# Moving a LayerNorm from the first stages of each pass into the merges of the same pass, by way of DRAM, with new ranks and filler matmuls

## The chip, the cores and the metric

One Trainium2 chip, all eight cores; each core computes one of the eight batch elements with the same program. The metric is the device time of the slowest core in microseconds (us). Some executions of any kernel here are in a slower state, in which the cores of one die or of both are granted a lower matrix-engine clock (0.87 on one die and 0.985 on the other in one slow run of the changed kernel). Ratios are the mean time of one kernel's fast runs over that of the other's of the same rounds, so they are not quite the ratio of the medians.

## The reference, cut to what matters

```python
def hybrid_layer(x, ...):                       # two layers, x is (8, 2048, 2048)
    h = x * (1 + scale) + shift                 # mixer input
    proj = h @ w_in
    ys = (ssd_branch(...), swa_branch(...), shortconv_branch(...), rglru_branch(...))
    m = sum_k sigmoid(proj_gate[k] + b_gate[k]) * (ys[k] @ w_branch[k])
    out = m @ w_out
    return layer_norm(ALPHA * x + gate * out, ln_w, ln_b)
```

## The kernel before

The kernel is a list scheduler written in Python. Parts of the computation are generators that add operations with a rank ("key"); the program simulates the five engines and the DMAs, always takes the ready operation of lowest rank, and so fixes the order of instructions on each engine. The traces show each engine keeping to one order (in the trace of this kernel ACT's 4518 and POOL's 563 instructions come in the same sequence on all eight cores, DVE's 6902 but for two swapped pairs of neighbours on a core at most): where the program believes that a DMA lands earlier than it does, the engine stands at the instruction that needs the data.

A core makes four passes: layer 1 on the first and second half of the sequence, then layer 2 on both. A pass has the stages short convolution and recurrence (the "first stages"), SSD (the state-space branch), attention, merges, output projection. While a pass merges its branches, the mixer input of the next pass is made in eight chunks (`h_chunk`). After the output projection come the statistics of the norm, and then, during the first stages of the *next* pass, the norm itself:

```python
def out_unit(n):
    ...
    for dc in range(NKC):                        # 16 blocks of 128 channels x 1024 tokens
        r, rr, tr = alloc([TU], F32)
        R[dc] = (r, tr.r, tr)                    # kept in SBUF until normalised
        ... yield from out_mm(...)               # r = x + gate * (m @ w_out), and sums
    ... ln_stats(part, rs, ms)
    for dc in range(NKC):
        ln_apply(l, u, dc, 0, TU, R[dc], rs, trs.r, ms, tms.r)   # 2 DVE, 1 ACT, 1 store
        yield P.key + LNSTEP                     # one every 7 us of rank
def h_chunk(n, j, direct):
    ...
        P.dma("sp", xt, src[u, kc], ...)         # src = x1, the normalised input of layer 2
        P.key += HL                              # rank what uses it HL later
        for h, b in enumerate((b0, b1)):
            act(o[b], xt[:, h * T:(h + 1) * T], AF.Identity, ..., scale=..., bias=...)
```

The softmax here doesn't subtract the row's maximum and nothing guards it: scores larger than these inputs give would overflow.

## Time and profile before

| | |
|---|---|
| time, median of 3 | 5880.87 us (5874.19 to 5884.1) |
| profiled execution | 5853.3 us, 5822.8 to 5853.3 over the cores |
| matrix engine (PE) busy | 5497.7 us |
| vector engine (DVE) busy | 4178.1 us |
| bytes moved by DMA | 856.94 MB |

The lines are in the prediction. ACT is the scalar engine, POOL is GpSimd, and SP is the sync engine, which issues most of the DMAs (1238 of 1728 in the trace of the kernel before). A row of a cut by stretches has, after the stretch, its length, then busy microseconds of PE, weight loads, DVE, ACT and POOL with instruction counts, then the granted clock, the busy share of the 16 DMA engines and GB/s.

### The profile page before, as it was taken

The page shows a single profiled execution, that of the slowest core. Times are in us where ns is not written, and L with a number is a line of the kernel's source. Part 1 is how long each engine was busy: PE and PEld are TensorE (multiplying, and loading weights), DVE is VectorE, ACT ScalarE, POOL GpSimd, SP SyncE. Part 2 cuts the span into 40 slices and gives each one's busy share as a digit, 9 for nine tenths or more (in the row PEclk, how much of TensorE's full clock was granted, in tenths as well). Part 3 has the DMA queues.
Part 4 walks back from the last instruction along what each step waited for, and adds up shares of the span by engine and source line. Part 5 has one row for each costly group of instructions (what it writes and reads, how often), then busy time and mean ns, then how long its engine had stood idle before and what let it go on. Part 6 is the DMA issues. An engine that isn't in the chain of part 4 may idle for free.

```text
span 5853.3 us, 84743 instructions; the slowest of 8 cores (5822.8 to 5853.3 us)
## 1 busy us (share of the span) xinstructions
PE 5497.7 (94%) x28129; PEld 2545.5 (43%) x28680; DVE 4178.1 (71%) x6902; ACT 2835.4 (48%) x4518; POOL 322.9 (6%) x563
## 2 busy tenths in 40 slices
PE   1999899899999999989999999999999999999998
PEld 1444344444444444444443444444444444444445
DVE  7787776666698788766578776766658777766556
ACT  1565654433266566443236566644324656645224
POOL 0000000000000000000000000000000000000004
PEclk9999999999999999999999999999999999999999
DMA  9567777576576677767566666766856556665554
GB/s 306 115 129 142 134 141 162 132 181 158 176 176 130 137 143 142 162 159 168 143 194 155 122 123 123 130 131 143 181 163 168 107 93 116 114 140 119 127 116 151
DMA packets 251823, 856.94 MB, mean 146 GB/s; under 512 B 27776, under 2 KB 91392, under 8 KB 206848
## 3 DMA queue, kind: packets, MB, share of 16 engines
q0 software_dynamic: 64672, 411.20, 40.7%
q1 hardware_dynamic: 184416, 423.51, 24.1%
q10 hardware_dynamic: 2304, 16.78, 0.9%
q8 instruction: 234, 3.83, 0.3%
q14 instruction: 197, 1.61, 0.1%
HBM read 1133.32 MB, written 120.85 MB: 214 GB/s over the span
## 4 chain that ended last, share of the span: by engine, by line
PE 78%; DMA 10%; DVE 5%; issue 4%; ACT 3%; SPq 1%; DVEq 0%; ACTq 0%; POOL 0%; POOLq 0%
PE ps L736 77%; DVE arena L709 3%; ACT arena L705 3%; DMA arena<-cum_scr 2%; DVE arena L713 2%; DMA arena<-arena 2%; DMA yd_scr<-arena 1%; DMA arena<-w_ada 1%; DMA arena<-wb 1%; PE ps L741 1%; DMA arena<-w 1%; DMA arena<-x 1%; SPq L329 1%; DMA arena<-x_scr 1%; ACT L705 0%
## 5 line engine op out<-in xcount | busy, mean ns | idle before, releaser
L736 PE MATMUL ps<-arena 128*128 128x512 bf16 (+6 forms) x27425 | 5472.5, 363 | 328.9 <-DVE arena L713 103.9
L736 PEld LDWEIGHTS ps<-arena 128*128 128x128 bf16 (+4 forms) x27976 | 2487.0, 100 | 3223.8 <-issue 612.5
L709 DVE TENSOR_TENSOR arena<-arena 128x1024 bf16<-128x1024 bf16 (+8 forms) x3052 | 1998.6, 693 | 297.2 <-ACT arena L705 176.5
L705 ACT ACTIVATE arena<-arena 128x512 f32<-128x512 f32 (+9 forms) x2356 | 1395.6, 633 | 1383.3 <-DVE arena L709 789.4
L709 DVE TENSOR_TENSOR arena<-ps,arena 128x512 f32<-128x512 f32 (+5 forms) x1491 | 708.9, 494 | 536.6 <-PE ps L736 469.4
L705 ACT ACTIVATE arena<-ps 128x512 f32<-128x512 f32 (+5 forms) x838 | 533.7, 644 | 666.8 <-PE ps L736 556.4
L713 DVE SCALAR_TENSOR_TENSOR arena<-arena 128x1024 f32<-128x1024 f32 (+2 forms) x765 | 760.1, 1009 | 92.4 <-ACT arena L705 56.7
L713 DVE SCALAR_TENSOR_TENSOR arena<-arena,ps 128x512 f32<-128x512 f32 (+1 forms) x640 | 405.9, 645 | 508.8 <-PE ps L736 428.6
L705 ACT ACTIVATE ps<-ps 128x512 f32<-128x512 f32 x624 | 363.7, 583 | 525.2 <-PE ps L736 492.6
L705 ACT ACTIVATE arena<-ps,arena 128x512 f32<-128x512 f32 (+1 forms) x456 | 311.9, 684 | 325.1 <-PE ps L736 297.5
L705 ACT ACT_TABLE_LOAD x238 | 305.4, 1283 | 89.9 <-DVE arena L709 38.6
L329 POOL DMA_DIRECT2D arena<-w x184 | 97.7, 531 | 2635.7 <-PE ps L736 1986.6
L713 DVE SCALAR_TENSOR_TENSOR arena<-ps,arena 128x512 f32<-128x512 f32 (+1 forms) x153 | 104.7, 687 | 157.3 <-PE ps L736 156.4
L329 POOL DMA_DIRECT2D arena<-wg x128 | 67.7, 529 | 1999.4 <-PE ps L736 1908.1
L709 DVE TENSOR_TENSOR ps<-ps,arena 128x512 f32<-128x512 f32 (+1 forms) x222 | 147.6, 665 | 14.1 <-DVE arena L713 0.5
L741 PE MATMUL ps<-arena 128*128 128x128 bf16 (+1 forms) x704 | 101.0, 243 | 10.2 <-DVE arena L709 5.3
L329 POOL DMA_DIRECT2D arena<-wb x128 | 67.9, 531 | 730.3 <-DVE arena L709 357.4
L741 PEld LDWEIGHTS ps<-arena 128*128 128x128 bf16 (+1 forms) x704 | 69.4, 115 | 67.2 <-issue 26.1
L709 DVE TENSOR_TENSOR arena<-arena,ps 128x256 f32<-128x256 f32 (+1 forms) x172 | 75.3, 450 | 22.0 <-PE ps L736 18.1
L727 DVE RECIPROCAL arena<-arena 128x4 f32<-128x4 f32 (+3 forms) x144 | 72.3, 504 | 15.0 <-ACT arena L705 8.5
L709 POOL TENSOR_TENSOR arena<-arena 128x256 f32<-128x256 f32 (+1 forms) x81 | 71.4, 907 | 95.0 <-ACT arena L705 94.4
L1604 DVE TENSOR_TENSOR_SCAN arena<-arena 128x1024 f32<-128x1024 f32 x32 | 74.1, 2317 | 0.5
(18 smaller groups left out, 85.1 us busy)
## 6 DMA issues: line engine op xcount, KB each, us to landing
arena<-w POOLq DMA_DIRECT2D x184, 1024.0 KB, 10.1
arena<-wg POOLq DMA_DIRECT2D x128, 1024.0 KB, 10.1
arena<-w_ada SPq DMA_DIRECT2D x128, 512.0 KB, 8.0
arena<-wb POOLq DMA_DIRECT2D x128, 512.0 KB, 10.6
arena<-x SPq DMA_DIRECT2D x64, 512.0 KB, 5.8
mp_scr<-arena SPq DMA_DIRECT2D x64, 512.0 KB, 8.6
arena<-cum_scr SPq DMA_DIRECT2D x128, 256.0 KB, 7.5
arena<-mp_scr SPq DMA_DIRECT2D x64, 512.0 KB, 9.9
```

What stands on the lines that cost most here:

```text
L329: eng.dma_start(out=o.fn[0], in_=o.fn[1]).then_inc(s, 16)
L705: return P.op("act", lambda e: e.activation(out=out, in_=in_, func=func, **kw), reads, writes, cost=cost, acc=acc, tbl=tbl, hi=hi)
L709: return P.op(eng, lambda e: e.tensor_tensor(out=out, in0=in0, in1=in1, op=op), reads, writes, cost=0.2 + n * 2.1e-3 if eng == "pool" else ...
L713: return P.op("dve", lambda e: e.scalar_tensor_tensor(out=out, in0=in0, scalar=scalar, in1=in1, op0=op0, op1=op1), reads, writes, cost=c_d ...
L727: P.op("dve", lambda e: e.reciprocal(out=out, in_=in_), reads, writes, cost=0.13 + n * 6.3e-3)
L736: r = e.matmul(out, lhsT=lhsT, rhs=rhs, start=st, stop=sp_, skip_group_check=True)
L741: P.op("pe", lambda e: e.transpose(out=out, in_=in_, identity=ident), reads, writes, cost=cost, acc=acc)
L1604: P.op("dve", lambda e: e.tensor_tensor_scan(out=c, data0=a, data1=xs, initial=init, op0=ALU.mult, op1=ALU.add), [ra, rxs] + ri, cv.r, cos ...
```

## The change

The intent is to take the norm of the pass before out of the first stages, where DVE is busiest, and put it into the merges, where the next mixer input is made. The unnormalised blocks go to DRAM at once and their SBUF is free. The scale (128 x 1024 fp32) lies meanwhile in the SSD state buffer, which is not used between the last SSD of one pass and the first of the next; for one pass the state is saved to DRAM and fetched back. The change also retunes ranks and adds filler matmuls that should keep the PE clock up. Core of the diff:

```diff
@@ out_unit
-            R[dc] = (r, tr.r, tr)
+            P.dma("sp", raw[n, dc], r, reads=tr.r, writes=[rRAW[n][dc]], nbytes=524288)
+            mem.free(tr)
-        for dc in range(NKC):
-            ln_apply(l, u, dc, 0, TU, R[dc], rs, trs.r, ms, tms.r)
+        for i, (v, r) in enumerate(((rs, trs.r), (ms, tms.r))):
+            P.dma("sp", lns[n, i], v, ...)
@@ h_chunk, layer 2
+                for h, b in enumerate((b0, b1)):
+                    xt, rx, tx = alloc([T], F32)
+                    P.dma("sp", xt, raw[n - 2, kc][:, lo], ..., nbytes=262144, hi=4.0)
+                    P.key += HL
+                    normalise(0, n - 2, kc, xt, rx, h * T, T)             # 2 DVE, 1 ACT
+                    P.dma("sp", x1[u, kc][:, lo], xt, ..., nbytes=262144)
+                    act(o[b], xt, AF.Identity, ...)
+    def ln_out(m): ...    # pass 3's norm, whose result is the output, in pass 4's merges
-    ROPEL, HL, ADAL = 0.0, 6.0, 15.0
+    ROPEL, HL, ADAL = 4.0, 10.0, 15.0
+    order = P.warm(order, ...)    # bursts of 3 filler matmuls into idle banks, in gaps
+                                  # that the program's own simulation shows
... (cut: loading and freeing the scale, spacing constants, bookkeeping)
```

## The prediction

> **What bounds the kernel now.** I read the page's busy shares first, then the chain that ended last, then busy time by stage, then the waits inside the stages that lose time, and last the clock.
>
> ```profile
> span 5853.3 us, 84743 instructions; the slowest of 8 cores (5822.8 to 5853.3 us)
> PE 5497.7 (94%) x28129; PEld 2545.5 (43%) x28680; DVE 4178.1 (71%) x6902; ACT 2835.4 (48%) x4518; POOL 322.9 (6%) x563
> PE 78%; DMA 10%; DVE 5%; issue 4%; ACT 3%; SPq 1%; DVEq 0%; ACTq 0%; POOL 0%; POOLq 0%
> ```
>
> The matrix engine (PE) is the bound: 94% busy, 78% of the chain. All that a change of elementwise work or buffers can win is its idle time, 5853.3 - 5497.7 = 356 us, and the time it runs on a slowed clock. The program makes four passes (two layers by two halves of the sequence), each with five stages: short convolution and recurrence, SSD, attention, merges, output projection. Cut at these stages (columns: busy us of each engine with its count, granted clock, DMA share, GB/s):
>
> ```profile
> 150.00:470.00 320.00, 317.55 (x1504) 139.22 (x1533) 247.31 (x361) 186.57 (x263) 16.43 (x31) 1.00 0.64 125
> 1155.00:1460.00 305.00, 296.04 (x1536) 137.58 (x1566) 188.40 (x343) 101.74 (x152) 15.30 (x29) 0.99 0.74 171
> 1460.00:1595.00 135.00, 133.66 (x614) 60.81 (x623) 77.69 (x110) 26.02 (x42) 1.05 (x2) 1.00 0.55 178
> 1595.00:1905.00 310.00, 301.20 (x1407) 131.52 (x1437) 281.10 (x356) 196.21 (x275) 12.68 (x24) 1.00 0.68 150
> 3028.00:3345.00 317.00, 304.94 (x1415) 132.89 (x1444) 268.30 (x343) 198.46 (x265) 15.79 (x30) 0.99 0.65 139
> 4450.00:4765.00 315.00, 310.74 (x1450) 135.63 (x1479) 256.35 (x304) 200.07 (x279) 13.73 (x26) 1.00 0.57 113
> 5450.00:5745.00 295.00, 293.58 (x1345) 133.83 (x1370) 157.07 (x240) 69.30 (x106) 19.51 (x30) 1.00 0.54 135
> ```
>
> Rows 1, 4, 5 and 6 are the first stage of passes 1 to 4. Pass 1 has no norm to apply; passes 2 to 4 apply the norm of the pass before. DVE rises from 247 to 281 us (91% of the stage) in pass 2, and PE idle goes from 2.5 us to 8.8, 12.1 and 4.3 us. The merges (rows 2 and 7) leave DVE at 62% and 53%. So the norm sits where DVE is scarcest, but it costs PE only about 25.2 - 3 x 2.5 = 18 us in all three passes.
>
> What the extra DVE work is shows in the groups of pass 2's first stage; its first-pass counterpart has 15 such instructions, not 46:
>
> ```profile
> L709 DVE TENSOR_TENSOR arena<-arena 128x1024 f32<-128x1024 f32 x46 | 56.0, 1229 | 2.3 <-ACT arena L705 2.3
> ```
>
> The rest of the idle time lies elsewhere. The same arithmetic on the cuts of the other stages gives 107 us in the four SSD stages, 53 us in attention, 23 in the merges, and 123 us before the first dense matmul. In attention DVE stands still behind the DMAs that turn halves of q and k for the rotary embedding, and PE behind DVE (first row from the waits of 2345 to 2600, the others DVE and PE in order of time):
>
> ```profile
> DVE arena L709 <- DMA arena<-arena: 12.7, 5, 7.8
> 2581.32 1.23 DVE L709 TENSOR_TENSOR arena<-arena 128x1024 f32<-128x1024 f32 x1 [7.75 <-DMA arena<-arena]
> 2583.49 6.86 PE L736 MATMUL ps<-arena 128*128 128x65 bf16 x30 [8.22 <-DVE arena L709]
> 2578.50:2585.00 6.50, 1.51 (x11) 0.88 (x12) 3.68 (x7) 0.00 (x0) 0.00 (x0) 0.50 0.67 241
> ```
>
> The last row is a cut inside that wait: the granted clock is 0.50. The clock record has 21 such stretches of 3.41 to 10.24 us between 500 us and 5430 us, each after a PE gap. Counting the columns of the matmuls that started in them, at half speed against full, gives 47 us lost.
>
> [...] stretches are multiples of 3.41 us, and dense 128x512 matmuls start 216 ns apart at full clock. [...] The trace has 1229 and 688 to 691. It follows that cutting a 1024-wide operation in two costs 0.15 us. [...] The trace has a 128 KB on-chip copy at 5.7 us to landing[...].
>
> **The change part by part.**
> (1) Norm out of the first stages. Removed from passes 2 to 4 each: 32 DVE operations x 1.225 = 39 us, 16 ACT operations x 1.16 = 19 us, 16 stores of 512 KB. It also ends the hold on 16 tiles of 4 KB per partition across the boundary. Gain on PE: the 18 us above, and the one slowed stretch at 3100 us, 2.4 us. Together -20 us.
> (2) Norm into the merges. Merges of passes 2 and 3 gain 64 half-width operations x 0.69 = 44 us of DVE each, and 32 ACT operations x about 0.70 = 22 us. DVE goes from 188 to about 232 of 305 us, 76%, well below the 91% above. They also get 8.4 MB of stores of the normalised input; the load of it is only swapped for the raw one. The hardware queue's 24.1% of 5853 us for 423.5 MB is 3.33 us of all 16 engines per MB, so 28 us, and the share goes from 0.74 to 0.83. Pass 4's merges get 39 us DVE and 16.8 MB, share 0.54 to 0.73. DVE works in order, so a late raw load can block it and with it the merge arithmetic; but these operations are ranked 10 instead of 6 behind their load. I put +2 us a pass, +6 us.
> (3) Raw stores in the output stages: 8.4 MB, 28 us of all engines in 133, so the share goes from about 0.57 to 0.78 beside the loads of w_out, x and h. Nothing waits for these stores. +2 us. Statistics and the saved state add 6.8 MB in all, nothing.
> (4) The state buffer holds the scale only between the last SSD of one pass and the first of the next. Its save and restore are off the path. 0.
> (5) Retuned ranks: the rotary multiplications are ranked 4 later. Their stalls above 3 us cost PE 3.2 + 3.3 + 4.5 + 8.2 = 19 us and 11 us in slowed clock. In the built order the typical distance on DVE from writing q to rotating it hardly grows (about 12 to 13 instructions); only the shortest (1 and 2) go to 5. I count a third of 30: -10 us.
> (6) Filler matmuls. The order of the changed program has 240 more 128x512 matmuls, in 80 bursts of 3: 47 bursts before the dense work and 33 later. A burst is 0.65 us at 216 ns, so at most 33 x 0.65 = 21 us if the gaps they were planned for are not there on the chip. I found some 35 gaps of over 1.4 us in the trace; the 33 bursts stand in 18 places. If half of the places meet a real gap, each saves about 2.2 us (47/21), so -20, and half of the bursts cost 11. Net -9 us. In the opening the slowed stretch at 131 to 151 us cost 2.1 us: -2 us.
> Sum: -20 + 6 + 2 - 10 - 9 - 2 = -33 us, 0.6%. 5881 - 33 = 5848; I say 5846.
>
> **The rivals.** (a) Nothing shows: PE's idle time moves with the schedule. All instructions are placed anew, and the SSD gaps (107 us, several behind loads of the cumulative decay and not touched by the change) may fall either way by 20 us. That gives 5860 to 5885. For it: the moved work was mostly hidden already. (b) The merges become the new jam: DVE blocked by raw loads that land late at share 0.83, weights of the merges late for PE. PE already waited for such weights at 630 and 876 us. A 5 us stall in each of 8 chunks x 2 passes would be +80 us, giving 5930. Against it: DVE at 76%, loads issued ahead, and before the same loads of x held ACT up in the merges for only 2.5 us. (c) The fillers work better than I think and the attention stalls vanish: -20 - 30 - 35, giving 5790. Against it: the fillers stand where the program expects gaps, and the largest gaps come from DMAs that land later than it expects.
>
> **Range and chances.** Predicted 5846 us, 8 times in 10 within 5800 to 5890. Faster by over 2% means below 5763, which would need 118 us, a third of all idle time and far beyond the parts above: 0.05. Slower by over 2%, above 5998, needs (b) in full: 0.03. Within 2%: 0.92.
>
> **What would show it.** Right if: DVE busy in the first stages of passes 2 to 4 falls by about 39 us each and PE idle there to 2 to 4 us; DVE in the merges rises to about 76% with PE idle there at most 3 us more a pass; bytes rise by some 40 MB; fewer than 18 slowed stretches; waits of DVE for the rotary DMAs shrink. Wrong if: PE in the merges waits for weights or for DVE behind raw loads, if slowed stretches stay at 21 while PE gains 20 us of busy time (fillers in gaps that are not there), or if the SSD gaps move by more than the rest together.

The sum stays -20 + 6 + 2 - 10 - 9 - 2 = -33 us, and its 1.225, 0.69 and 1.16 us an operation and 216 ns a matmul are measured in the trace. "1229 and 688 to 691" are ns of an fp32 TENSOR_TENSOR of 1024 and of 512 columns. On the clock the trace of the kernel before (core 6) shows this: each of the 21 slowed stretches begins 0.6 to 4.8 us after the start of a PE gap of 1.7 us or more, and 128x512 matmuls start 427 ns apart in such stretches (median) against 216 outside. That a filler in a gap saves the stretch was my estimate from that, not shown.

## The result, and the profile after

The fast runs of the changed kernel took 5893.61 and 5904.16 us (two more, 5960 and 6502 us, were slow; the median of all four is 5932.12 us). Before took 5874.19 to 5884.1 us. The ratio is 1.0032 with a 95% interval of 1.0008 to 1.0056: slightly slower, where I had predicted 0.6% faster. It is within 2% all the same.

The page of the changed kernel, its busy and chain lines and the group of the fillers:

```profile
span 5892.1 us, 85799 instructions; the slowest of 8 cores (5850.3 to 5892.1 us)
PE 5575.6 (95%) x28361; PEld 2565.6 (44%) x28920; DVE 4178.1 (71%) x6966; ACT 2851.4 (48%) x4551; POOL 323.2 (5%) x563
PE 78%; DMA 11%; DVE 5%; issue 4%; ACT 2%; SPq 1%; DVEq 0%; ACTq 0%; POOL 0%; POOLq 0%
L2379 PE MATMUL ps<-arena 128*128 128x512 bf16 x229 | 81.5, 496 | 59.0 <-DVE arena L797 30.8
```

PE is "busier" only because of the fillers (81.5 us). The bound and the chain are nearly the same. Bytes rose by 41.0 MB, as forecast ("some 40"). Slowed stretches between 500 and 5430 us did not fall below 18: there are 28 on this core, and 22.5 in the mean over the cores against 20.9 before.

The cuts of the first stages of passes 2, 3 and 4, and of pass 2's merges with output; then pass 2's wide fp32 operations in its first stages, and its attention waits for the rotary copies:

```profile
1612.00:1922.00 310.00, 308.03 (x1449) 135.99 (x1476) 254.23 (x335) 181.84 (x263) 13.35 (x25) 1.00 0.62 134
3060.00:3377.00 317.00, 315.11 (x1476) 138.65 (x1504) 241.12 (x323) 184.06 (x255) 16.84 (x32) 1.00 0.63 127
4479.00:4794.00 315.00, 312.95 (x1463) 137.10 (x1492) 225.46 (x278) 183.37 (x265) 13.74 (x26) 1.00 0.49 94
2640.90:3060.70 419.80, 399.59 (x1912) 181.77 (x1949) 273.19 (x453) 132.97 (x201) 14.25 (x27) 0.98 0.82 204
...
L793 DVE TENSOR_TENSOR arena<-arena 128x1024 f32<-128x1024 f32 x15 | 18.3, 1220 | 1.3 <-ACT arena L789 1.3
...
DVE arena L793 <- DMA arena<-arena: 4.2, 4, 1.2
```

PE in the first stages went as predicted: idle 8.8 to 2.0 us, 12.1 to 1.9, 4.3 to 2.1. The 46 wide operations are 15. DVE's busy time fell from 281 to 254 us, 268 to 241 and 256 to 225, so by 27 to 31 us and not by 39: the wide operations that left pass 2 make up 37.7 us, so some 11 us of other DVE work moved in. The merges did not go as predicted. The same stretch of the kernel before, from pass 2's last attention matmul to its norm statistics:

```profile
2626.10:3027.80 401.70, 394.86 (x1922) 181.67 (x1958) 239.99 (x394) 109.78 (x170) 14.25 (x27) 1.00 0.68 172
```

It has grown by 18 us, DMA share rose from 0.68 to 0.82, and PE idle from 6.8 to 20.2 us though DVE is busy only 65% of the time. The waits of the changed kernel show why: first DVE's waits in this stretch, then DVE, ACT and PE in order of time around 2850 us, then the cut around it.

```profile
DVE arena L793 <- DMA arena<-raw_scr: 23.5, 8, 8.2
...
2855.78 0.69 DVE L793 TENSOR_TENSOR arena<-arena 128x512 f32<-128x512 f32 x1 [8.15 <-DMA arena<-raw_scr]
2857.76 0.81 ACT L789 ACTIVATE arena<-arena 128x512 f32<-128x512 f32 x1 [9.01 <-DVE arena L793]
2859.21 3.15 PE L820 MATMUL ps<-arena 128*128 128x512 bf16 x7 [6.34 <-ACT ps L789]
...
2840.00:2860.00 20.00, 12.58 (x69) 5.38 (x69) 11.85 (x23) 5.73 (x9) 1.05 (x2) 0.94 0.97 196
```

Read the three engines as one chain. DVE stood 8.15 us at one norm multiplication because its raw block had not landed. ACT waited 9.01 us for DVE, and PE 6.34 us for a bank of PSUM (`ps`, where it writes its output) with which ACT had not finished. The DMA engines were 97% busy in these 20 us; of what the trace shows, only they had no room left. A full stretch alone does not stop PE: two other cuts of 20 us, from 2700 and from 2820 us, have shares of 1.04 and 1.03 (a transfer is booked where it starts), and PE idle is 0.1 us in each.

To see the whole run I cut each core's trace at events that both kernels have: the statistics matmul that ends SSD, the last attention matmul, the statistics matmul of the norm. The table has the mean length over all eight cores of one profiled execution, in us; columns 3 to 6 belong to the experiments below.

| stretch | before | changed | e1 | e10 | e11 | e14 |
|---|---|---|---|---|---|---|
| pass 1 first stages + SSD | 914.6 | 923.2 | 915.3 | 928.3 | 926.0 | 919.1 |
| pass 2 first stages + SSD | 756.8 | 745.0 | 746.6 | 750.2 | 756.4 | 754.0 |
| pass 3 first stages + SSD | 736.4 | 725.6 | 726.2 | 728.4 | 737.2 | 740.5 |
| pass 4 first stages + SSD | 717.3 | 727.3 | 730.0 | 731.9 | 719.2 | 731.4 |
| attention, all passes | 1091.6 | 1094.1 | 1090.8 | 1094.5 | 1093.3 | 1096.2 |
| pass 1 merges + output | 399.4 | 401.2 | 400.7 | 399.6 | 400.4 | 399.3 |
| pass 2 merges + output | 399.3 | 414.1 | 413.7 | 401.1 | 415.3 | 399.3 |
| pass 3 merges + output | 398.9 | 418.6 | 421.9 | 408.5 | 412.7 | 398.1 |
| pass 4 merges | 345.7 | 340.2 | 340.2 | 340.2 | 345.7 | 345.6 |
| tail | 76.1 | 75.9 | 75.8 | 77.6 | 76.0 | 75.4 |
| whole | 5836.1 | 5865.2 | 5861.3 | 5860.1 | 5882.1 | 5859.1 |

So 22.5 us were won where the norm left (passes 2 and 3), and 34.5 us lost in the merges of the same passes. Pass 4 lost 10.0 us in its first stages with SSD, although the norm left it too.

A stretch does not hold the same matmuls in every layout. Counted in columns, at 216 ns for 512, the changed kernel has 5.2 us less work in pass 4's merges, 6.0 us more in pass 4's attention, 4.4 us more in pass 3's merges and 2.6 us less in pass 2's. So the 5.5 us by which pass 4's merges are shorter is work that moved out (e4, which has the new ranks and no moved norm, has the same 340.2 us there, and e3, which has the moved norm and the old ranks, has 345.7). Without the moved work the merges of passes 2 and 3 lost 17.4 and 15.3 us. e1 and e10 share one layout, e11 and the kernel before share another.

### The profile page after: what moved, and what is told of

Read it like the earlier page. It is cut to its first block, busy times and chain, and to the rows that moved or that the text cites. A ratio compares the mean times of both kernels' runs of the same rounds, so it can differ in the third digit from the quotient of the medians.

```text
span 5892.1 us, 85799 instructions; the slowest of 8 cores (5850.3 to 5892.1 us)
## 1 busy us (share of the span) xinstructions
PE 5575.6 (95%) x28361; PEld 2565.6 (44%) x28920; DVE 4178.1 (71%) x6966; ACT 2851.4 (48%) x4551; POOL 323.2 (5%) x563
## 4 chain that ended last, share of the span: by engine, by line
PE 78%; DMA 11%; DVE 5%; issue 4%; ACT 2%; SPq 1%; DVEq 0%; ACTq 0%; POOL 0%; POOLq 0%
PE ps L820 77%; DVE arena L793 3%; DMA arena<-cum_scr 2%; ACT arena L789 2%; DMA arena<-w_ada 2%; DVE arena L797 1%; DMA arena<-arena 1%; DMA yd_scr<-arena 1%; DMA arena<-x 1%; DMA arena<-raw_scr 1%; SPq L405 1%; PE ps L825 1%; DMA x_scr<-arena 1%; DMA arena<-yd_scr 1%; DMA mp_scr<-arena 1%
## 5 line engine op out<-in xcount | busy, mean ns | idle before, releaser
L820 PE MATMUL ps<-arena 128*128 128x512 bf16 (+4 forms) x27428 | 5475.0, 364 | 232.9 <-DVE arena L793 83.4
L820 PEld LDWEIGHTS ps<-arena 128*128 128x128 bf16 (+3 forms) x27976 | 2482.8, 100 | 3141.6 <-issue 526.1
L793 DVE TENSOR_TENSOR arena<-arena 128x1024 bf16<-128x1024 bf16 (+7 forms) x3116 | 1998.5, 679 | 355.4 <-ACT arena L789 182.0
L789 ACT ACTIVATE arena<-arena 128x512 f32<-128x512 f32 (+9 forms) x2388 | 1410.2, 629 | 1436.7 <-DVE arena L793 780.0
L789 ACT ACTIVATE arena<-ps 128x512 f32<-128x512 f32 (+4 forms) x838 | 535.1, 645 | 659.6 <-PE ps L820 566.4
L2379 PE MATMUL ps<-arena 128*128 128x512 bf16 x229 | 81.5, 496 | 59.0 <-DVE arena L797 30.8
## 6 DMA issues: line engine op xcount, KB each, us to landing
arena<-wb POOLq DMA_DIRECT2D x128, 512.0 KB, 11.3
```

Of the source, the lines that this page charges most:

```text
L789: return P.op("act", lambda e: e.activation(out=out, in_=in_, func=func, **kw), reads, writes, cost=cost, acc=acc, tbl=tbl, hi=hi)
L793: return P.op(eng, lambda e: e.tensor_tensor(out=out, in0=in0, in1=in1, op=op), reads, writes, cost=0.2 + n * 2.1e-3 if eng == "pool" else ...
L820: r = e.matmul(out, lhsT=lhsT, rhs=rhs, start=st, stop=sp_, skip_group_check=True)
L2379: r = e.matmul(ap, lhsT=IDB, rhs=MASK, start=True, stop=True, skip_group_check=True)
```

## The experiments

The theory after reading the two traces (A): the loss is in the merges, where engines that work in order wait for late DMAs. Rivals: (B) the fillers are the loss; (C) the fillers do their work and hide something worse; and within A, whether the order (A1: the program believes the load lands too early) or the traffic (A2: the DMA engines are full, so whatever is waited for is late) is what has to be mended. A rival to everything is that any new layout moves times by some 10 us.

### The parts, one at a time

**e1**, the changed kernel without fillers:

```diff
-    order = P.warm(order, [(banks[b], rbank[b]) for b in range(8)], keep, MMC)
```

> The changed kernel without its 240 filler matmuls; all else, the order of every other instruction too, stays. Theory A (the loss is in the merges, where DVE waits for raw loads; fillers cost what they win): within 12 us of the changed kernel, with the number of half-clock stretches after 500 us within 4 of its 28. Theory B (fillers are the loss: some 18 us of them lie in the body and they slow the opening): 15 to 25 us faster than the changed kernel, at or below the kernel before. Theory C (fillers do what they are for): slower by 8 us or more, and more half-clock stretches.

Ratio to before 1.0032 (1.0007 to 1.0057), the same as with fillers. In the profile its total is 3.9 us shorter than the changed kernel's. B falls, since e1 stays slower than before: the fillers are not the loss. Against C speaks the profile alone, as the two ratios leave some 20 us either way; half-clock stretches rose from 22.5 to 26.0 (mean over the cores), which C had forecast, but no time followed. The following runs build on e1, because its order is not mixed up with bursts.

**e2**, the kernel before with fillers only (the same `warm` and `keep` added):

> The kernel before with the filler matmuls planned for its own gaps, nothing else changed. Theory A: within 12 us of the kernel before, in either direction, opening stretch at half clock longer in the record but no faster. Theory B: 15 to 25 us slower than before. Theory C: 10 us or more faster, half-clock loss down from 44 us a core to below 30.

Ratio 0.9978 (0.9959 to 0.9998), a gain of 0.2%. Time lost to half clock on real matmuls (columns of the matmuls that start in such a stretch, at half speed against full, by the 427 and 216 ns above, mean over the cores) fell from 44.5 to 35.0 us. The 13 us are C's "10 us or more", 1 us beyond A's "within 12"; the half-clock time stayed above C's 30.

**e3**, the move of the norm alone, from e1:

```diff
-    ROPEL, HL, ADAL = 4.0, 10.0, 15.0
+    ROPEL, HL, ADAL = 0.0, 6.0, 15.0
-                          slack=3.5, nbytes=131072, acc=h > 0, hi=HI)      # copies of k
+                          nbytes=131072, acc=h > 0, hi=HI)
-            mg(k0 + TC + (M1S * dc - M1E if dc < LAZY else s2 * dc), dc, 1)
+            mg(k0 + TC + s2 * dc - (M1E if dc < LAZY else 0.0), dc, 1)
```

> The move of the norm alone: no fillers, the old ranks of the rotary and norm operations (norm in the merges ranked 6 instead of 10 behind its load), old spacing of the first merges. Theory A: the first stages and SSD of passes 2 and 3 are about 25 us shorter together than before, the merges with output of these passes are longer by at least 30 us, DVE waits for raw loads there of 20 us or more a pass; total 0 to +25 us against before. If the norm move is good in itself and only its company is bad (Theory B), it is 15 to 25 us faster than before.

Ratio 1.0075 (1.0052 to 1.0099), some 44 us slower than before. Mean over the cores: pass 2 and 3 first stages with SSD 747.4 and 726.4 us (won 9.4 and 10.0), merges with output 419.5 and 421.0 us (lost 20.2 and 22.1), pass 4's first stages with SSD 733.1 us (lost 15.8). On its slowest core DVE waited 55.5 us for raw loads, in 16 waits. The gain was 19 us where about 25 were expected, the loss 42 where at least 30 were, and the total missed its range (0 to +25 us) clearly: attention, too, took 14.2 us longer.

**e4**, the kernel before with the new ranks alone (the reverse of the lines above):

> The kernel before with the new ranks alone (rotary operations 4 later, the mixer input's operations 10 instead of 6 behind their load, key copies believed to land 1.5 us later, second early merge 3 us earlier). My prediction counted -10 us for this. Theory A (ranks change little: in the changed kernel attention took as long as before): within 8 us of before, attention stages within 3 us a pass.

Ratio 1.0018 (0.9993 to 1.0043): no gain. Attention moved by +2.2, -6.9, -1.5 and +16.5 us in the four passes, so "within 3 us a pass" missed, and the total of about +10 us missed "within 8". Of the 16.5 us, 11 are matmuls that moved into pass 4's attention; PE idle there rose by 3.5 us. Ranks shuffle, they don't win here. Beside the moved norm they do help: e1 is e3 with the new ranks, and 0.43% (about 25 us) faster, with 45.9 us of waits for raw loads instead of 55.5. In the profiles 15.0 us of that gain lie in attention and 4.9 in the merges with output of passes 2 and 3.

### Order or traffic?

**e5**, e1 with one number changed: the program believes the raw loads to land 7 us later.

```diff
-                    P.dma("sp", xt, raw[n - 2, kc][:, lo], ..., hi=4.0)
+                    P.dma("sp", xt, raw[n - 2, kc][:, lo], ..., hi=4.0, slack=9.0)
```

> The changed kernel without fillers, with one number changed: the program that lays out the order believes each raw load in the merges to land 7 us later than it did, so it puts the norm's multiplications later in the order of DVE. Bytes, instructions and buffers stay. Theory A1 (the merges of passes 2 and 3 lose because DVE, in order, stands at a multiplication whose raw load has not landed): waits of DVE for raw loads fall from some 20 us a pass to under 8, PE idle in the merges with output of passes 2 and 3 falls from 15 us each to under 7, total 15 to 25 us faster than the kernel without fillers. Theory A2 (the DMA engines are full, and loads of weights are late whatever the order): PE idle there stays above 12 us a pass, total within 8 us.

Ratio 1.0054 (1.0024 to 1.0083): not faster than e1, so A1 fails as a remedy. Its profiled execution was in the slow state, but the clock of cores 0 to 3 was not lowered to 0.81, the level of that state (0.813 to 0.816 on cores 0 to 3), in the merges of passes 2 and 3. On these four cores DVE waited only 6.8 to 11.6 us for raw loads in the whole run, as A1 wanted, yet the two stretches took 435.4 and 425.4 us (413.9 and 420.1 on the same cores of e1) and PE idle there was 32.6 and 18.6 us, where A1 forecast under 7 and A2 over 12. Sorted by the last DMA in the chain before each gap of PE over 0.6 us, 12.7 us of pass 2's gaps stood behind stores of the normalised input (x_scr), 7.0 behind stores of the mixer input (h_scr), and none behind raw loads. Run e9 has the same change, another layout and a fast profile.

**e9**, the changed kernel (with fillers), with that edit and the loads of the cumulative decay believed 4 us later:

> The changed kernel with its fillers, the raw loads believed to land 7 us later and the loads of the cumulative decay 4 us later. Theory A1: merges as in the run with the raw loads alone, and the SSD stages lose half of the ACT waits for the cumulative decay (some 80 us in all before); 30 to 50 us faster than the changed kernel, 10 to 30 us faster than the kernel before. Theory A2: within 10 us of the changed kernel.

Ratio 1.0014 (0.9985 to 1.0043): not separable from before, nor clearly from the changed kernel. The merges with output of passes 2 and 3 still took 410.1 and 422.3 us. Waits for raw loads and for stores on the slowest core, first e1 and then e9:

```profile
DVE arena L793 <- DMA arena<-raw_scr: 45.9, 15, 6.1
...
ACT arena L789 <- DMA x_scr<-arena: 28.4, 4, 9.1
...
ACT arena L789 <- DMA h_scr<-arena: 8.0, 1, 8.0
```

```profile
ACT arena L789 <- DMA h_scr<-arena: 22.1, 4, 7.2
ACT arena L789 <- DMA x_scr<-arena: 15.6, 3, 8.5
```

In e9 DVE waited only 6.8 us for raw loads, in 2 waits, but ACT's waits for the stores of the mixer input (h_scr) grew from 8.0 to 22.1 us: ACT wants to write a buffer that a store is still reading. Its waits for the stores of the normalised input fell from 28.4 to 15.6. ACT's waits for the cumulative decay fell too, from 90.2 to 10.8 us, which A1 had also asked for, and A1's gain of 30 to 50 us still did not come. Later places in the order removed the waits that they were meant for, and the time did not follow; in e5 the sorting shows it behind the stores.

**e7**, the kernel before with added stores, laid out anew:

```diff
+            if l:
+                for h in range(2):
+                    P.dma("sp", dup[u, kc][:, lo], xt[:, lo], reads=[rx], writes=[rDUP[u][kc]], nbytes=262144, acc=h > 0)
```

> The kernel before, with the traffic of the change alone: in the merges of passes 2 and 3 each loaded tile of the mixer input is also stored to a scratch tensor, in two halves, 8.4 MB a pass; the norm stays where it was. Theory A1: DMA share of these merges rises to about 0.83 or more, but PE idle there stays below 7 us a pass and the total within 8 us of before. Theory A2: PE idle rises to 10 us or more a pass and the total by 20 us or more.

Ratio 1.0063 (0.9999 to 1.0126). Pass 3's merges with output grew from 398.9 to 421.3 us and pass 2's from 399.3 to 403.2. PE idle rose to 20.0 us in pass 3, as A2 said, but only from 3.1 to 5.3 in pass 2, as A1 said. So this speaks for A2 by half; and pass 4, which has no added stores, lost 16.7 us in its first stages with SSD: the new layout mixes in. The next two runs keep the order fixed.

**e10**, e1 with every instruction in the same place on every engine, but the 64 stores of the normalised input shrunk to 8 columns. Its output is wrong, which doesn't matter for the time.

```diff
-P.dma("sp", x1[u, kc][:, lo], xt, ..., nbytes=262144, acc=h > 0)
+P.dma("sp", x1[u, kc][:, h * T:h * T + 8], xt[:, 0:8], ..., nbytes=262144, acc=h > 0)
-        src = x_in if l == 0 else x1        # residual, in both output stages
+        src = x_in
```

> The changed kernel without fillers, every instruction in the same order on every engine, but each of the 64 stores of the normalised input in the merges moves 8 columns instead of 512, so 16.8 MB of writes vanish (wrong result on purpose: the second layer takes its residual from the program's input, which has the same size). Theory A2 (the DMA engines are full in the merges, so everything that the in-order engines wait for lands late): waits of DVE for raw loads fall from 46 us to under 25, PE idle in merges with output of passes 2 and 3 falls from 15 us each to under 7, and these two stretches shorten by 15 us or more together. If the bytes do not matter and only the order does: idle there stays above 12 us each.

All that A2 expected came. The merges with output of passes 2 and 3 went from 413.7 and 421.9 us to 401.1 and 408.5, together -26.0 us; PE idle there from 14.9 and 15.4 to 5.9 and 6.4 us. The ratio to before is 0.9987 (0.9952 to 1.0021), against 1.0032 for e1. Cut of pass 2's merges with output, first e1 and then e10, and DVE's waits for raw loads in the whole run of e10 (e1's are above):

```profile
2619.90:3035.30 415.40, 397.70 (x1909) 181.56 (x1947) 273.02 (x454) 132.94 (x201) 14.23 (x27) 0.99 0.80 206
2648.40:3052.70 404.30, 396.75 (x1949) 181.16 (x1946) 272.65 (x454) 133.03 (x201) 14.25 (x27) 1.00 0.76 191
...
DVE arena L793 <- DMA arena<-raw_scr: 9.2, 4, 4.2
```

DVE does the same 273 us of work in the same order, and PE idle in this stretch is 7.6 us instead of 17.7. So most of the loss comes neither from the norm's arithmetic nor from its place in the order, but from the bytes: 26 of the 37.4 us by which e1's two stretches exceed those of the kernel before. The other 11 us no run assigns.

The bytes act in two ways that e10 does not part. Raw loads land sooner without them (median 7.9 us from issue, 10.6 in e1). And the stores themselves hold buffers: in pass 2's merges with output on the slowest core, ACT waited 22.0 us for stores of the normalised input in e1 and 11.4 in e10, DVE 21.5 and 4.7 for raw loads.

**e11**, the counterpart: the kernel before with its order fixed, and 64 stores from a constant buffer put into the DMA queue, two after each of the 32 stores of the mixer input.

```diff
+    for o in order:
+        out.append(o)
+        if o.idx in MARK:                  # a store of the mixer input, passes 2 and 3
+            for _ in range(2): ...         # 256 KB, constant SBUF -> scratch; no waits
```

> The kernel before with its order on every engine kept, and 64 stores of 256 KB from a constant buffer to a scratch tensor put into the DMA queue beside the stores of the mixer input in the merges of passes 2 and 3, 8.4 MB a pass. Nothing waits for them. The earlier run with such stores was laid out anew, and lost 17 us in pass 4 where it has no stores. Theory A2: merges with output of passes 2 and 3 get 5 to 15 us longer each, all other stretches stay within 3 us of before. If the loss of the earlier run was only the new order: every stretch within 3 us.

Ratio 1.0051 (1.0021 to 1.0080). Pass 2's merges with output +16.0 us (1 us above the range), pass 3's +13.8; all other stretches from pass 1's attention on within 3 us. (Pass 1's first stages, +11.4 us here and +13.7 in e10: on two cores of each, the clock record shows 0.81 for some 160 us. The mean matmul time lost to a lowered clock was 21 and 20 us there instead of 11; this makes up most of the difference.) ACT's waits for loads of the normalised input in pass 2's merges with output, first before, then e11, with e11's cut:

```profile
ACT arena L705 <- DMA arena<-x_scr: 3.6, 3, 1.7
```

```profile
ACT arena L708 <- DMA arena<-x_scr: 25.8, 8, 8.1
...
2644.70:3066.60 421.90, 402.22 (x1961) 182.89 (x1958) 239.92 (x394) 109.82 (x170) 14.24 (x27) 0.98 0.76 183
```

Stores that nobody waits for, 8.4 MB a pass, make the loads that ACT does wait for come late, and cost 29.8 us, nearly as much as the change lost in its merges (34.5). But e11 adds two things, and the traces show that the second counts. From issue to landing these loads hardly changed (mean over the cores 9.7 to 10.8 us in pass 2, 10.4 to 10.3 in pass 3); they were issued later, and the sync engine spent 84 us of pass 2's stretch on issuing DMAs instead of 42 (86 instead of 39 in pass 3). So e11 does not tell bytes from the longer list of the sync engine; e11 with tiny stores would, and was not run. e10 does: its 64 stores stay in the list (73 us of issuing in each of the two stretches, 78 and 73 in e1), and only their bytes go. A2 is shown by e10 for the bytes. Whether the loads wait for the 16 engines or behind the stores in their own queue is open; the merge weights, on GpSimd's queue (wb), landed 1.2 us sooner in e10 (median 11.3 instead of 12.5), so not all of it is the queue.

**e8**, the changed kernel with every DMA believed 3 us later (`SLACK = 5.0`):

> The changed kernel with its fillers, where the program that lays out the order believes every DMA to land 3 us later (margin 5 instead of 2 us). If late landings are what moves PE idle time in this kernel (Theory A1, for raw loads, cumulative decay and rotary copies alike), PE idle outside the opening falls from 136 us by 30 us or more and the kernel is 20 to 50 us faster than the changed one, below the kernel before. If not, within 10 us, or slower because buffers are held longer.

A clear miss: ratio 1.0137 (1.0107 to 1.0166). The program now planned more gaps and put 124 us of fillers into them instead of 73, and PE idle outside the fillers still rose from 275.3 to 292.9 us in all. Of the 63.4 us by which the profile is longer (mean over the cores), 50 are fillers and 18 idle, less 5 of other matmul time. Why the idle time rose is not shown.

**e12** and **e13**, the chunks of the next mixer input spread over more of the merges, without and with fillers:

```diff
-    HS0, HSTEP = 45.0, 24.0
+    HS0, HSTEP = 40.0, 30.0
```

> The changed kernel without fillers, with the eight chunks of the next mixer input 30 us apart instead of 24 in the merges, so raw loads and stores spread over 240 us instead of 192. Theory A2: peaks of DMA share fall, waits of DVE for raw loads fall below 30 us, PE idle in the merges of passes 2 and 3 falls by 4 us or more each, total 8 to 20 us faster than the kernel without fillers. If it is the order alone: anything within 10 us, with waits as before.

> The same spreading with the fillers, as a candidate that could beat both kernels: 5 to 15 us below the run without fillers if the fillers win here what they won on the kernel before (13 us), so 0 to 20 us below the kernel before. If fillers win nothing in this layout, as they did in the changed kernel, equal to the run without them.

Ratios 1.0074 (1.0049 to 1.0099) and 1.0050 (1.0022 to 1.0078): wrong direction. Pass 2's and 3's merges with output in e12 took 423.8 and 431.8 us, idle 23.3 and 23.7. Waits for raw loads fell to 32.3 us on the slowest core, a little short of the forecast. By the sorting of PE's gaps, raw loads are still the largest group (6.7 us in pass 2, 9.3 in pass 3), followed by h_scr stores (6.1 us in pass 3), DVE with no late DMA just before (5.5 us in pass 2) and x_scr stores (4.3 us in pass 2). The fillers of e13 did win the 14 us that were expected of them, but not against the kernel before. Why more room in time made it worse is not shown.

### What is good in the change, and pass 4

**e14**, the kernel before with one third of the change: only pass 3's norm, whose result goes into no mixer, moves into pass 4's merges. **e15** adds the fillers; **e16** is e2 again.

```diff
+            if n == 2:
+                P.dma("sp", raw[dc], r, ...); mem.free(tr)      # in out_unit
+        if n == 2: ...store the scale and shift; return         # instead of ln_apply
+    def ln_out(): ...                                           # in pass 4's merges
```

> The kernel before with one third of the change: only the norm of pass 3, whose result is the output and goes into no mixer, is moved into the merges of pass 4; passes 1 and 2 keep theirs; no fillers, old ranks. DMA share in the merges of pass 4 was 0.54, so it should have room for 16.8 MB. Theory A2: merges of pass 4 no longer than before by more than 3 us, first stages with SSD of pass 4 up to 6 us shorter, total 0 to 8 us faster than before. If pass 4 loses 10 us in its first stages here too, the loss there is of the moved norm itself (its raw stores or freed buffers), not of what the passes before it left.

> The same with the fillers, as the candidate that keeps what the runs showed to be good: 10 to 20 us faster than before, at or a little below the run with fillers alone (ratio 0.9978).

> The kernel before with fillers alone once more, on the same chip as the two others, because its gain of 0.22% is near what different orders alone move: ratio again between 0.996 and 0.9995. If it is 1.000 or above, the gain was the chip's and the fillers win nothing.

Ratios: e14 1.0009 (0.9989 to 1.0029), e15 1.0015 (0.9993 to 1.0036), e16 0.9992 (0.9963 to 1.0022). The gains expected of e14 (0 to 8 us) and e15 (10 to 20) did not come; e16 lies in its range. In e14 pass 4's merges took what they did before (345.6 us), so this norm has DMA room there. But its first stages with SSD took 14.1 us more. A cut of the first stages and of SSD of pass 4, before and then e14 (on the core that lost most there):

```profile
4449.00:4855.00 406.00, 400.90 (x1887) 176.53 (x1926) 317.73 (x392) 254.84 (x371) 17.42 (x33) 1.00 0.57 111
4855.00:5167.00 312.00, 301.44 (x1615) 142.47 (x1646) 248.38 (x454) 211.13 (x411) 14.51 (x28) 1.00 0.67 123
```

```profile
4454.00:4860.00 406.00, 403.07 (x1903) 178.41 (x1941) 286.07 (x365) 238.11 (x356) 17.95 (x34) 1.00 0.52 95
4860.00:5194.00 334.00, 307.73 (x1597) 143.91 (x1627) 246.91 (x451) 213.15 (x409) 13.99 (x27) 0.96 0.59 115
```

The first stages did gain (PE idle 5.1 to 2.9 us). SSD lost (10.6 to 26.3 us), with hardly any change in DVE or ACT work and less DMA. By what I had put on record for e14, a loss here would be of the moved norm itself, its raw stores or its freed buffers. But e7 lost the same there without moving any norm. In five runs laid out anew (changed, e1, e3, e7, e14) the first stages with SSD of pass 4 took 10 to 17 us more; in e4 they took 0.9 us more and in e9 1.9 us less. So the layout of pass 4's SSD in the kernel before was a good one that many new layouts don't hit. That it is only the layout is the reading that fits these runs; I did not fix the order there to prove it.

No version beat both kernels beyond doubt. Fillers on the kernel before (0.9978, then 0.9992) are the best; the second interval includes no gain.

## Why the prediction was wrong, point by point

- **What bounds it, and step (1), the first stages: right for passes 2 and 3.** PE idle in the first stages alone fell by 19.2 us in three passes, where I had counted 18; with SSD, passes 2 and 3 won 22.5 us, which includes what fillers and ranks did there. For pass 4 the sum was wrong: its first stages gained about what they could (2 us), but SSD behind them lost more.
- **Step (2), the merges: this is the step that failed.** I put "+2 us a pass, +6 us"; it measured +14.8 and +19.7 us in passes 2 and 3 (17.4 and 15.3 without the matmuls that moved), and no gain or loss in pass 4. My arithmetic for the load was near: over the first 268 us after the last attention matmul of pass 2 the share went from 0.73 to 0.87 (I had 0.74 to 0.83 for 305 us) and DVE from 61% to 70% (62% to 76%). But I read such a mean share as room, and looked at DVE, which had it. In the 20 us windows around the longest waits it was 0.95 and more. e10 shows that the bytes of the stores of the normalised input, which I had listed and then not charged, are most of the cost: 26 us for 16.8 MB, by loads that land late and by buffers that the stores hold. This was my rival (b), against which I had argued with the waits of a kernel that did not have those stores.
- **Step (3), raw stores in the output stages: nothing seen against it.** Pass 1's merges with output, which has raw stores but no moved norm, grew by 1.7 us (in e3 it shrank by 0.9).
- **Step (4), the state buffer: nothing seen against it.** No wait for its save or restore stands among the long ones.
- **Step (5), ranks, -10 us: not additive.** On the kernel before they win nothing (e4). Beside the moved norm all new ranks together are worth about 25 us (e3 to e1), 15.0 of them in attention, but against an attention that had grown by 14.2 us; which rank does it was not tested. The long rotary stall of pass 2 did vanish (12.7 to 4.2 us of waits), others stayed.
- **Step (6), fillers, -11 us: not there.** e1 equals the changed kernel. My sign of being wrong came true: PE gained 78 us of busy time and the slowed stretches did not fall. On the kernel before they won 13 us and 5. In the opening of the changed kernel the short bursts did not hold the clock up: PE was busy 71.8 us of the first 150 (26.8 before), 144 fillers stand in the trace there, and the granted clock was 0.75, with seven stretches at half clock from 38 to 154 us. The fillers took 496 ns each on average over the run. (The clock record of the kernel before starts only at 128 us, so the two openings can't be compared.)
- **Rival (a)**, that PE's idle time moves with any new layout, was right in size: pass 4's first stages with SSD moved by 10 to 17 us in five runs. My range should have been as wide on the slow side as (b) with half its force.

- **Slips in the sums.** The parts of (c) give 5796 us and not 5790, and 5846 stands for a sum of 5848; neither matters. The on-chip copies of 128 KB, for which I gave the median of 5.7 us, landed in 2.2 us at the least, and later where the DMA engines were busier: the third of them whose 10 us around the issue had the lowest DMA share (up to 0.50) in 2.3 us in the median, the third with the highest (0.81 and more) in 7.5.

The loss of about 29 us in the profiles (mean over the cores) is then: -22.5 (first stages with SSD, passes 2 and 3), +34.5 (merges with output, the same passes), +10.0 and -5.5 (pass 4; the -5.5 is moved work), +8.6 (pass 1's first stages with SSD, within what that stretch varies by between these runs), +2.5 attention (which took in 3.3 us of moved work), and +1.5 from pass 1's merges and the tail.

## What to carry to other kernels

Before moving work into a stage that looks idle, ask which of its resources is scarce there: here the receiving stage had vector time to spare and no DMA time, and a mean DMA share of 0.82 already meant late landings (the changed kernel's 256 KB raw loads took 11.6 us in the median). Bytes were not free here, even in stores whose data nobody needed soon (26 us for 16.8 MB, e10 against e1): they delayed loads and held buffers, and correcting the order of one wait brought out the next (from e1 to e9 DVE's raw-load waits went from 45.9 to 6.8 us, ACT's waits for h_scr stores from 8.0 to 22.1). A fixed-order experiment that takes the bytes away settles this where any re-laid schedule is blurred by 10 us of luck. The counterpart that adds bytes needs a control with tiny transfers, since issuing them also takes time (84 us of the sync engine instead of 42 in e11). And before two layouts are compared by stage, count whether the stages hold the same work.
